# Latent attention: the second key block's values as one product of whole 32-bit operands, and the next head's transposes directly behind the values' product

## The chip, the cores and the metric

The kernel runs on one core of a Trainium2 chip. The metric is the device time of one execution in microseconds (us). The engines are TensorE (PE: matrix products and transposes; PEld: its weight loads), VectorE (DVE), ScalarE (ACT), GpSimd (POOL) and SyncE (SP, which issues the DMAs). Each engine works off its own queue in order and waits on semaphores of the others.

## The reference

A decoder trunk of two layers on 256 tokens of width 1024, all in float32. Layer 0 has a forgetting attention, layer 1 a multi-head latent attention. Around each stand two half-step feed-forward blocks and an input embedding, and behind each part a layer norm. What the change touches is the latent attention of layer 1:

```python
def mla_mixer(x, w_dq, q_norm, w_uq, w_o, k_nope, k_rope, v, cos, sin):
    c_q = rms_norm(x @ w_dq, q_norm)
    q = jnp.einsum('bsc,chd->bshd', c_q, w_uq)
    q_nope = q[..., :QK_NOPE_DIM]
    q_rope = rope(q[..., QK_NOPE_DIM:], cos[:, None, :], sin[:, None, :])
    scale = (QK_NOPE_DIM + QK_ROPE_DIM) ** -0.5
    ...
    # for each block of 128 queries, against the keys up to them:
    s = (einsum('bqhd,bkhd->bhqk', qn, k_nope) + einsum('bqhr,bkr->bhqk', qr, k_rope)) * scale
    w = jax.nn.softmax(where(k_pos <= q_pos, s, -inf), axis=-1)
    o = jnp.einsum('bhqk,bkhd->bqhd', w, v)
    ...
    return o.reshape(B, S, MLA_HEADS * V_HEAD_DIM) @ w_o
```

There are 16 heads with values of width 128, and two blocks of 128 queries. The first block of queries sees the first 128 keys, the second block sees all 256. So of the transposed probabilities there are three 128x128 blocks a head: first keys by both blocks of queries (256 columns), and second keys by the second block of queries (128 columns).

## The kernel before, in words

**Split operands.** A float32 matrix is kept as two parts of the type fp32r: the high part is a copy through that type, the low part is the rest (`parts`, L496 to 500: ScalarE copies, VectorE subtracts). A product is then three passes of TensorE: high by high, high by low, low by high (`mm3`, L481). Weights come by DMA into `raw` and are split in the same way (`Stream.split`: ScalarE writes the high part, VectorE the low part; lines L193, L194, L201, L205).

**The order.** The latent attention (`mla`, L1226) is a list of steps, `ORDER` (L47), run one after the other by the loop at L1504. Each step puts its instructions at the end of the queues of the engines it uses, so the list is the order on every engine. `f n`, `a` and `l` are the weight splits that are put between the steps. The steps that matter, for head h:

- `gen h`: query and key of head h by products with the weights (15 passes of 256 columns), and their split into `qk`.
- `QK h`: the scores of head h into a PSUM bank of the ring `tr` (two banks), ten passes.
- `sm h`: the softmax without its division. VectorE reduces (L1420), ScalarE takes the exponentials into `P` (L1425).
- `div h 0`: VectorE takes reciprocals (L1434) and multiplies both blocks of `P` by them (L1437).
- `T h`: three transposes of `P` on TensorE (L450), and the split of the result into the one tile `PT` (L452).
- `AV h`: the product of values and probabilities (L1462): three passes of 256 columns for the first keys, three of 128 columns for the second keys. Its result is split into `ot`.
- `O h t`: the output projection of head h for the token block t: six passes of 512 columns.
- `V g t`: the values of four heads for the key block t: six passes of 512 columns, and ScalarE's copy of the high part (L1270). `vlo g t` is VectorE's subtraction for the low part (L1275).
- `rc`, `rot`, `zs`, `zU`: rotation, split and transposes of the rotary queries, partly on POOL.

`T h` can run when `div h 0` is done, `AV h` when the split of `PT` is done. `PT` has one buffer, so `T h` follows `AV h-1` in any order.

Of the kernel before, what the change touches and what calls it, by code (L numbers as in the profile page):

```python
# [10 lines left out]
F32 = mybir.dt.float32  # L11
F32R = mybir.dt.float32r
AF = mybir.ActivationFunctionType
# [33 lines left out]
ORDER = (  # L47
# [26 lines left out]
)  # L74


# [14 lines left out]
class Recorder:  # L91
# [10 lines left out]
    lend = reclaim = check = load = busy = pair = split = split_pieces = ahead = later = split_now = fill = pump  # L102
    between, hl, hold = {}, {}, False
# [293 lines left out]
class Trunk:  # L397
# [828 lines left out]
    def mla(self, li):  # L1226
        nc, S, a = self.nc, self.S, self.a
# [4 lines left out]
        v = {}  # L1232
# [26 lines left out]
        vps = {}  # L1259

        def V(g, t):
            w = self.use(("kvv", g))
            ps = vps[g, t] = self.bank(("h", "y", "tr")[VRING[g][t]])
            for k in range(2):
                self.mm3(
                    ps, lambda i: self.ckv[:, i, 256 * k + 128 * t : 256 * k + 128 * t + 128],
                    lambda i: w[:, i, 512 * k : 512 * k + 512], k == 0, k == 1,
                )
            o = v[t, g] = self.tl([128, 2, 512], F32R, "g4", 5)
            nc.scalar.activation(o[:, 0, :], ps, AF.Copy)  # L1270
            S.busy(act=512)

        def vlo(g, t):
# [70 lines left out]
        zT = self.xT.rearrange("p t i k c -> p (t i k c)").rearrange("p (h c) -> p h c", c=256)  # L1344
# [34 lines left out]
        st, PT = {}, {}  # L1379
# [66 lines left out]
        def T(h):  # L1446
            P = st.pop(h)
            b = self.bank("tr")
            for i in range(3):
                self.transpose(b[:, 128 * i : 128 * i + 128], P[:, 128 * i : 128 * i + 128])  # L1450
            o = self.tl([128, 2, 384], F32R, "PT", 1)
            self.parts(o[:, 0, :], o[:, 1, :], b[:, 0:384])
            PT[h] = o

        OT = []

        def ot_of(h):
            if h >= 14:
                return self.kvt[:, 512 * (h - 14) : 512 * (h - 13)].rearrange("p (i c) -> p i c", i=2)
            return OT[h >= 10][:, (h + 2 * (h >= 10)) % 4]  # L1460

        def AV(h):  # L1462
            if h in (0, 10):
                OT.append(self.own([128, 4, 2, 256], F32R, "ota" if h else "otb"))
            o = PT.pop(h)
            ps = self.bank("h")
            g, c = h // 4, 128 * (h % 4)
            for m, (i, jj) in enumerate(((0, 0), (0, 1), (1, 0))):
                self.mm(
                    ps[:, 0:256], v[0, g][:, i, c : c + 128], o[:, jj, 0:256], m == 0, False  # L1470
                )
            for m, (i, jj) in enumerate(((0, 0), (0, 1), (1, 0))):
                self.mm(
                    ps[:, 128:256], v[1, g][:, i, c : c + 128], o[:, jj, 256:384], False, m == 2
                )
            ot = ot_of(h)
            self.parts(ot[:, 0, :], ot[:, 1, :], ps[:, 0:256])

        y = [[None] * 2 for _ in range(2)]
# [14 lines left out]
        def hold(x):  # L1494
            S.hold = bool(x)

        steps = dict(
            dq=dq, rms=rms, dqs=dq_scale, cqT=cq_transpose, V=V, vlo=vlo, qr=q_rope, rope=rope, rc=rope_copy, rot=rotate, zT=zT_first,
            zs=z_split, zU=zT_last, gen=gen, QK=QK, sm=softmax, div=divide, T=T, AV=AV, O=O, y=room, hold=hold,
            f=S.fill, a=S.ahead, l=S.later, XT=lambda t, n: self.XT(t, (n,)),  # L1500
            exp=lambda: self.ready_for(AF.Exp), gb=lambda: self.load_gb(li, 1),
            lend=lambda: S.lend("qk"), ln=lambda t: self.ln(t, y[t], ALPHA, LN_EPS),
# [119 lines left out]
```

## Time and profile before

| what | us |
|---|---|
| median of three runs (1078.75 to 1079.87) | 1078.85 |
| the profiled execution, its own time | 1081.3 |
| its span, first to last instruction | 1079.5 |
| TensorE busy in the span | 1063.7 |
| VectorE busy | 719.1 |
| ScalarE busy | 543.7 |
| POOL busy | 73.2 |

The mean granted clock of TensorE was 0.997 of full speed. The latent attention's heads lie between about 740 and 850 us of the span. In the timeline a row gives the start in us, the time from the first start to the last end of the instructions merged in it, the engine, the line, the operation, output and input, and the count; in brackets stands the idle time before it and what ended it. Matmuls are pipelined: the time between two starts is the cost of one, and it is shorter than the duration shown. Loads of weights overlap the matmuls.

### The profile page before, as it was taken

How to read it: one execution, taken by the hardware profiler on the slowest of the kernel's cores; microseconds unless marked ns; L12 is line 12 of the kernel's file. 1: busy time of each engine (PE TensorE's matmuls, PEld its weight loads, DVE VectorE, ACT ScalarE, POOL GpSimd, SP SyncE). 2: the span in 40 equal slices, each digit the busy share in tenths (PEclk: the TensorE clock that was granted, in tenths of full speed). 3: DMA queues.
4: the chain of work that ended last, by engine and by line, in shares of the span. 5: the costliest groups of instructions: out<-in, count | busy, mean ns of one | idle time of the engine just before them, and what ended most of it. 6: DMA issues, size and time to landing. Idle time of an engine off the chain costs nothing.

```text
span 1079.5 us, 17532 instructions
## 1 busy us (share of the span) xinstructions
PE 1063.7 (99%) x7236; PEld 973.4 (90%) x7236; DVE 719.1 (67%) x1043; ACT 543.7 (50%) x805; POOL 73.2 (7%) x104
## 2 busy tenths in 40 slices
PE   9999999999999999999999999999999999999997
PEld 8989998899889999998899999988899789898986
DVE  6675545888897545548966554388777886455566
ACT  5564433667646434444555443336576465444431
POOL 0000000223200000000320000012100000000000
PEclk9999999999999999999999999999999999999998
DMA  8785642543348655454477554322444468555502
GB/s 297 288 313 207 252 167 81 198 179 130 119 167 303 233 190 193 142 196 161 164 270 273 188 190 158 108 93 106 145 145 164 180 226 311 186 207 189 185 11 78
DMA packets 33091, 199.58 MB, mean 185 GB/s; under 512 B 3698, under 2 KB 5490, under 8 KB 12148
## 3 DMA queue, kind: packets, MB, share of 16 engines
q1 hardware_dynamic: 33012, 198.47, 51.4%
q8 instruction: 57, 0.93, 0.3%
q14 instruction: 22, 0.18, 0.0%
HBM read 197.40 MB, written 1.05 MB: 184 GB/s over the span
## 4 chain that ended last, share of the span: by engine, by line
PE 89%; DVE 6%; ACT 2%; issue 1%; POOL 1%; DMA 0%; SPq 0%; DVEq 0%; POOLq 0%; ACTq 0%
PE y L489 32%; PE h L489 32%; PE tr L489 22%; DVE hl L194 2%; PE tr L493 2%; DVE x L569 1%; ACT hl L193 1%; DVE st L551 0%; DVE x L550 0%; DMA raw<-in_w_dram 0%; PE h L493 0%; ACT P L1425 0%; DVE PT L499 0%; PE tr L1065 0%; DVE g L798 0%
## 5 line engine op out<-in xcount | busy, mean ns | idle before, releaser
L194 DVE TENSOR_TENSOR hl<-raw,hl 128x1024 fp32r<-128x1024 f32 (+3 forms) x268 | 316.0, 1198 | 150.4 <-ACT hl L193 149.6
L193 ACT ACTIVATE hl<-raw 128x1024 fp32r<-128x1024 f32 (+3 forms) x268 | 269.8, 1028 | 184.9 <-PE y L489 98.4
L489 PE MATMUL y<-hl,g 128*128 128x512 f32 x816 | 190.7, 390 | 0.0
L489 PE MATMUL h<-xT,hl 128*128 128x256 f32 x1560 | 188.6, 280 | 1.4 <-ACT hl L231 0.5
L489 PEld LDWEIGHTS h<-xT,hl 128*128 128x128 f32 x1560 | 184.2, 191 | 3.5 <-ACT xT L498 0.9
L489 PEld LDWEIGHTS y<-hl,g 128*128 128x128 f32 x816 | 152.0, 188 | 30.7
L489 PE MATMUL tr<-xT,hl 128*128 128x256 f32 x1512 | 176.6, 277 | 0.0
L489 PEld LDWEIGHTS tr<-xT,hl 128*128 128x128 f32 x1512 | 174.2, 188 | 0.5
L489 PE MATMUL h<-hl,xT 128*128 128x512 f32 (+2 forms) x300 | 67.8, 374 | 0.4 <-DVE xT L499 0.4
L489 PE MATMUL y<-hl,xT 128*128 128x512 f32 (+3 forms) x360 | 65.4, 334 | 0.0
L489 PEld LDWEIGHTS h<-hl,xT 128*128 128x128 f32 x300 | 53.2, 188 | 10.7 <-DVE xT L499 1.0
L489 PEld LDWEIGHTS y<-hl,xT 128*128 128x128 f32 x360 | 55.5, 188 | 6.3 <-ACT xT L498 0.4
L561 POOL TENSOR_TENSOR rs<-ve,mhalf 128x1 f32<-128x1 f32 x16 | 15.2, 951 | 601.3 <-DVE ve L560 601.3
L489 PE MATMUL y<-hl,otb 128*128 128x512 f32 x168 | 43.3, 399 | 0.7 <-DVE hl L194 0.5
L499 DVE TENSOR_TENSOR g<-P,g 128x512 fp32r<-128x512 f32 x38 | 26.3, 692 | 26.5 <-ACT g L498 26.5
L498 ACT ACTIVATE xT<-tr 128x512 fp32r<-128x512 f32 x28 | 16.1, 597 | 49.3 <-PE tr L493 49.3
L498 ACT ACTIVATE g<-P 128x512 fp32r<-128x512 f32 x38 | 24.0, 632 | 32.3 <-DVE P L678 32.3
L489 PEld LDWEIGHTS y<-hl,otb 128*128 128x128 f32 x168 | 30.2, 188 | 7.1 <-DVE hl L194 0.8
L194 DVE TENSOR_TENSOR otb<-raw,otb 128x1024 fp32r<-128x1024 f32 (+1 forms) x20 | 24.1, 1203 | 17.3 <-ACT otb L193 17.3
L677 ACT ACTIVATE P<-tr 128x512 f32<-128x512 f32 x20 | 12.0, 600 | 42.8 <-PE tr L489 42.8
L194 DVE TENSOR_TENSOR qk<-raw,qk 128x1024 fp32r<-128x1024 f32 (+1 forms) x21 | 25.7, 1222 | 11.7 <-ACT qk L193 11.7
L678 DVE TENSOR_TENSOR P<-P,tr 128x512 f32<-128x512 f32 x20 | 13.7, 687 | 28.6 <-PE tr L489 17.0
(264 smaller groups left out, 1414.8 us busy)
## 6 DMA issues: line engine op xcount, KB each, us to landing
raw<-in_ffn_in_dram SPq DMA_DIRECT2D x85, 1024.0 KB, 5.0
raw<-in_ffn_out_dram SPq DMA_DIRECT2D x44, 1024.0 KB, 5.0
raw<-in_pg_dram SPq DMA_DIRECT2D x8, 1024.0 KB, 4.8
raw<-in_mo_dram SPq DMA_DIRECT2D x8, 1024.0 KB, 4.8
raw<-in_kq_dram SPq DMA_DIRECT2D x8, 640.0 KB, 4.0
gb<-in_ln_g_dram SPq DMA_DIRECT2D x8, 512.0 KB, 5.8
gb<-in_ln_b_dram SPq DMA_DIRECT2D x8, 512.0 KB, 6.8
raw<-in_fk_dram SPq DMA_DIRECT2D x4, 1024.0 KB, 4.9
```

The source lines that it names most:

```text
L193: nc.scalar.activation(hi, src, AF.Copy)
L194: nc.vector.tensor_tensor(lo, src, hi.bitcast(F32), op=ALU.subtract)
L489: self.nc.tensor.matmul(out, lhsT, rhs, start=start, stop=stop)
L493: self.nc.tensor.transpose(out, in_, self.ident)
L498: self.nc.scalar.activation(hi, src, AF.Copy)
L499: self.nc.vector.tensor_tensor(lo, src, hi.bitcast(F32), op=ALU.subtract)
L561: nc.gpsimd.tensor_tensor(rs, ve, self.mhalf, op=ALU.pow)
L569: nc.vector.scalar_tensor_tensor(xs, xs, rs if i else mv[:, 0:1], self.gb[:, i, c0:c1], op0=ALU.mult if i else ALU.subtract, op1=ALU.add i ...
L677: nc.scalar.activation(gt, ps[0], AF.Silu)
L678: nc.vector.tensor_tensor(gt, gt, ps[1], op=ALU.mult)
```

## The change

For the second key block, the values stay one plain float32 tile (`V g 1` copies its bank once, and the four steps `vlo g 1` are gone). `T h` splits only the first 256 columns of the transposed probabilities; VectorE copies the last 128 columns as plain float32 into `raw`, which lies in the place of an older tile, `negc`. `AV h` keeps its three passes of 256 columns and then issues one product of the two plain float32 operands in place of three passes of 128 columns.

In `ORDER`, `T h+1` now stands directly behind `AV h` for every head (with `zU 1 1` between them for head 8). Where the two were apart, either `AV h` moved back to the place of `T h+1` (heads 1, 10 and 11: `AV 1` behind `QK 3` and `gen 4`; `AV 10` behind `gen 13`, with `T 11` ahead of `QK 12`; `AV 11` behind `gen 14`), or `T h+1` moved forward (`T 2` ahead of `O 0 0`, `T 3` ahead of `gen 5`, `T 4` ahead of `zU 0 0` and `gen 6`, `T 5` ahead of `O 3 1` and `gen 7`, `T 8` ahead of `gen 10`, `T 9` ahead of `gen 11`, `T 10` ahead of `gen 12`, `T 14` ahead of `O 6 1` and `QK 15`, `T 15` ahead of `O 8 1`, with `O 7 1` now ahead of `AV 14`). The order in the queues of DMAs and of POOL is the same as before, and so is all work outside the latent attention.

```diff
@@ ORDER, the stretch from QK 2 to QK 7 @@
     "f 4", "QK 2", "f 2", "zs 1 0", "y", "sm 2", "a", "f 3", "div 2 0", "O 0 1", "f 1",
-    "AV 1", "f 4", "QK 3", "gen 4", "f 1", "O 0 0", "T 2", "sm 3", "a", "div 3 0", "l", "O 1 0", "O 1 1",
-    "AV 2", "f 4", "a", "f 3", "gen 5", "T 3", "f 4", "l", "QK 4", "sm 4", "f 1", "f 1", "div 4 0", "f 1", "f 3",
-    "f 1", "f 4", "O 2 1", "O 2 0", "AV 3", "f 2", "zU 0 0", "gen 6", "T 4", "a", "QK 5", "sm 5", "f 2", "div 5 0",
-    "f 2", "l", "f 3", "O 3 0", "f 1", "V 2 1", "vlo 2 1", "f 4", "AV 4", "f 4", "O 3 1", "l", "gen 7", "T 5", "a",
+    "f 4", "QK 3", "gen 4", "f 1", "AV 1", "T 2", "O 0 0", "sm 3", "a", "div 3 0", "l", "O 1 0", "O 1 1",
+    "AV 2", "T 3", "f 4", "a", "f 3", "gen 5", "f 4", "l", "QK 4", "sm 4", "f 1", "f 1", "div 4 0", "f 1", "f 3",
+    "f 1", "f 4", "O 2 1", "O 2 0", "AV 3", "T 4", "f 2", "zU 0 0", "gen 6", "a", "QK 5", "sm 5", "f 2", "div 5 0",
+    "f 2", "l", "f 3", "O 3 0", "f 1", "V 2 1", "f 4", "AV 4", "T 5", "f 4", "O 3 1", "l", "gen 7", "a",
     "QK 6", "sm 6", "f 2", "O 4 1", "div 6 0", "l", "f 1", "O 4 0", "f 4", "zU 1 0", "AV 5", "f 4", "T 6", "a",
...
@@ ORDER, the end @@
     "gen 15", "AV 12", "T 13", "sm 14", "f 1", "div 14 0", "l", "O 12 0",
-    "AV 13", "O 6 1", "f 3", "QK 15", "f 3", "T 14", "f 4", "lend", "O 13 0", "sm 15", "f 1", "f 1",
-    "div 15 0", "l", "AV 14", "O 7 1", "hold 0", "O 8 1", "hold 1", "f 3", "gb", "f 1", "T 15", "O 9 1",
+    "AV 13", "T 14", "O 6 1", "f 3", "QK 15", "f 3", "f 4", "lend", "O 13 0", "sm 15", "f 1", "f 1",
+    "div 15 0", "l", "O 7 1", "AV 14", "T 15", "hold 0", "O 8 1", "hold 1", "f 3", "gb", "f 1", "O 9 1",
     "AV 15", "O 14 0", "hold 0", "f 5", "f 3", "O 15 0", "ln 0",
...
@@ def V(g, t) @@
-            o = v[t, g] = self.tl([128, 2, 512], F32R, "g4", 5)
-            nc.scalar.activation(o[:, 0, :], ps, AF.Copy)
+            if t:
+                o = v[t, g] = self.tl([128, 512], F32, "g4", 5)
+                nc.scalar.activation(o, vps.pop((g, t)), AF.Copy)
+            else:
+                o = v[t, g] = self.tl([128, 2, 512], F32R, "g4", 5)
+                nc.scalar.activation(o[:, 0, :], ps, AF.Copy)
@@ def T(h) @@
             o = self.tl([128, 2, 384], F32R, "PT", 1)
-            self.parts(o[:, 0, :], o[:, 1, :], b[:, 0:384])
-            PT[h] = o
+            raw = self.tl([128, 384], F32, "negc", 1)[:, 0:128]
+            self.parts(o[:, 0, 0:256], o[:, 1, 0:256], b[:, 0:256])
+            nc.vector.tensor_copy(raw, b[:, 256:384])
+            S.busy(dve=128)
+            PT[h] = o, raw
@@ def AV(h) @@
-            for m, (i, jj) in enumerate(((0, 0), (0, 1), (1, 0))):
-                self.mm(
-                    ps[:, 128:256], v[1, g][:, i, c : c + 128], o[:, jj, 256:384], False, m == 2
-                )
+            self.mm(ps[:, 128:256], v[1, g][:, c : c + 128], raw, False, True)
+            S.busy(pe=128)
```

More of the change, by code (lines that the diff above doesn't have):

```diff
@@ L1464, in AV @@
                 OT.append(self.own([128, 4, 2, 256], F32R, "ota" if h else "otb"))
-            o = PT.pop(h)
+            o, raw = PT.pop(h)
             ps = self.bank("h")
```

47 rows, old and new, of the table ORDER are left out of this document.

## The prediction

> **What bounds the kernel now.** I read the page's busy times and chain first, then the busy time of each engine stretch by stretch, then the timelines of the three stretches in which TensorE is not full.
>
> ```profile
> span 1079.5 us, 17532 instructions
> PE 1063.7 (99%) x7236; PEld 973.4 (90%) x7236; DVE 719.1 (67%) x1043; ACT 543.7 (50%) x805; POOL 73.2 (7%) x104
> PE 89%; DVE 6%; ACT 2%; issue 1%; POOL 1%; DMA 0%; SPq 0%; DVEq 0%; POOLq 0%; ACTq 0%
> ```
>
> TensorE is the bound: a matmul taken out in a full stretch is time won. The next rows are stretches (us: length, then busy time of PE, PEld, DVE, ACT, POOL) of the latent attention.
>
> ```profile
> 744.00:762.00 18.00, 14.42 (x97) 12.22 (x97) 14.35 (x26) 11.59 (x28) 12.91 (x10) 1.00 0.36 131
> 762.00:832.00 70.00, 70.00 (x494) 65.09 (x493) 55.16 (x135) 44.91 (x104) 0.00 (x0) 1.00 0.41 141
> 832.00:847.00 15.00, 14.40 (x83) 11.76 (x82) 10.77 (x25) 8.76 (x20) 0.00 (x0) 1.00 0.40 141
> ```
>
> In the heads from 762 to 832 TensorE never waits. Before that it loses 3.6 us, after it 0.6 us. So a new wait in the middle costs its whole length, and a matmul saved inside an early wait earns nothing.
>
> **The price of the new values' product.** AV(h) drops three 128-column passes on split operands and issues one product of whole 32-bit operands. The kernel has one such product: the warm-up at L465, 384 columns.
>
> ```profile
> 1.20 0.50 PEld L465 LDWEIGHTS y<-mask 128*128 128x128 f32 x2 [1.20 <-POOL mhalf L449]
> 1.21 1.65 PE L465 MATMUL y<-mask 128*128 128x384 f32 x2 [1.21 <-POOL mhalf L449]
> 2.65 1.06 PE L493 MATMUL tr<-ident 128*128 128x128 f32 x4
> 786.30 0.60 PE L493 MATMUL tr<-ident,ota 128*128 128x128 f32 x4
> ```
>
> One instruction became two weight loads and two passes, and the next one started 1.44 us after it. The two groups of transposes show that everything at the start runs at half speed: 1.06 us for four against 0.60. So 128 columns cost at most 1.44 / 3 / 2 = 0.24 us. The lower end is two weight loads.
>
> ```profile
> 774.14 0.41 PEld L489 LDWEIGHTS tr<-qk 128*128 128x128 f32 x3
> 774.47 0.30 PEld L489 LDWEIGHTS tr<-fs,xT 128*128 128x128 f32 x2
> 786.63 0.77 PEld L489 LDWEIGHTS h<-PT,g 128*128 128x128 f32 x6
> 787.34 0.32 PEld L493 LDWEIGHTS tr<-ident,P 128*128 128x128 f32 x3
> ```
>
> Three 128-column passes take 0.33 us from load to load (774.14 to 774.47), six of AV 0.71. Two loads are 0.22 us, so the new product costs 0.22 to 0.24 and replaces 0.33 to 0.35: 0.09 to 0.13 won a head. I take 0.10, from the cleaner 128-column row. Heads 0 and 1 end ahead of waits that other engines set (below), so 14 heads count: **-1.4 us** (-1.3 to -1.8).
>
> The Trainium skill, "FP8 and Floating Point Precision", section "TensorE Precision Notes", has true FP32 as four passes through the array. The two 384-column passes agree if each makes two of them; a reader who takes it as four loads has the third rival.
>
> **VectorE and ScalarE.**
>
> ```profile
> L1275 DVE TENSOR_TENSOR g<-y,g x3: 678/679/683, 729.7 to 752.5; 128x512 fp32r<-128x512 f32 x3
> L499 DVE TENSOR_TENSOR PT<-tr,PT 128x384 fp32r<-128x384 f32 x16 | 8.8, 550 | 0.3 <-ACT PT L498 0.2
> L233 DVE CAST hl<-raw x1: 293/293/293, 3.8 to 3.8; 128x256 fp32r<-128x256 f32 x1
> ```
>
> Four low parts of second-block values go (4 x 0.68). Each T's subtraction shrinks from 384 to 256 columns (about 0.41) and a copy of 128 is added (under the 0.29 of 256; I take 0.2): +0.06 to +0.12 a head. VectorE gains about 1.3 us in all, off the bound. The one removed ahead of a wait, before T 0, doesn't end it: the division of P does, and that stands in front. ScalarE's copy shrinks by a third, hidden. DMAs, SP's and POOL's queues keep their order.
>
> **The moved transposes.** T(h) needs head h's divided P, and its work used to sit behind a score product, a `gen` (1.8 us) or an `O` (1.4 us). Now it follows AV(h-1), and everything behind it on TensorE waits with it. I went through each head: QK(h), what TensorE has until T(h), and when VectorE ends the division.
>
> *T 2.* AV 1 leaves its place ahead of QK 3, T 2 overtakes O 0 0.
>
> ```profile
> 754.75 3.73 DVE L194 TENSOR_TENSOR hl<-raw,hl 128x512 fp32r<-128x512 f32 x2
> 758.53 1.10 PE L489 MATMUL h<-gb,hl 128*128 128x256 f32 x7 [0.98 <-DVE hl L194]
> 759.46 1.55 PE L489 MATMUL y<-hl,otb 128*128 128x512 f32 x6
> 760.45 0.77 DVE L1437 TENSOR_SCALAR P<-P,su 128x128 f32<-128x128 f32 x2
> 761.11 0.61 PE L493 MATMUL tr<-ident,P 128*128 128x128 f32 x3
> 761.47 0.70 PE L489 MATMUL y<-hl,otb 128*128 128x512 f32 x2
> ```
>
> VectorE's two splits end at 758.5 and hold gen 4, whose end at 759.46 stays; so does the division (760.45 on). Before, O 0 0 ran from 759.46 and T 2 came almost without a wait. After, AV 1 fills 0.6 us, TensorE stands until 761.1, and O 0 0's 1.4 us comes behind. **+1.5 us** (1.3 to 1.6). T 3 and T 4 overtake gen 5 and gen 6; reckoned on from there, AV(h-1) ends within 0.1 to 0.2 us of the division: **+0.2** (0 to 0.5).
>
> *T 5* overtakes O 3 1 and gen 7.
>
> ```profile
> 775.39 1.56 PE L489 MATMUL y<-hl,otb 128*128 128x512 f32 x6
> 777.54 1.57 ACT L193 ACTIVATE hl<-raw 128x1024 fp32r<-128x1024 f32 x2
> 778.17 0.80 PE L489 MATMUL h<-PT,g 128*128 128x256 f32 x6
> 778.62 1.23 DVE L194 TENSOR_TENSOR hl<-raw,hl 128x1024 fp32r<-128x1024 f32 x1 [0.85 <-ACT hl L193]
> 778.81 1.59 PE L489 MATMUL y<-hl,otb 128*128 128x512 f32 x6
> 779.96 0.55 DVE L1437 TENSOR_SCALAR P<-P,su 128x128 f32<-128x128 f32 x2
> 782.04 0.49 PE L493 MATMUL tr<-ident,P 128*128 128x128 f32 x3
> ```
>
> QK 5 ended at 775.39 (O 3 0 begins there), AV 4 at 778.81 (O 3 1 begins). The division starts at 779.96 because a split stands in front of it on VectorE, which itself waits for ScalarE behind the exponentials. P's first block is out about 0.28 later, 4.85 us after QK 5; PT of head 4 now comes earlier and gives 0.4 back. That is 4.45 against 3.3 us of TensorE work: **+1.1** (0.9 to 1.5). T 9 and T 10, by the same reckoning: **+0.4** (0.1 to 0.7).
>
> *T 14* overtakes O 6 1 and QK 15.
>
> ```profile
> 834.96 0.80 PE L489 MATMUL h<-PT,g 128*128 128x256 f32 x6
> 835.60 1.59 PE L489 MATMUL y<-hl,otb 128*128 128x512 f32 x6
> 836.33 0.55 DVE L1437 TENSOR_SCALAR P<-P,su 128x128 f32<-128x128 f32 x2
> 838.18 0.49 PE L493 MATMUL tr<-ident,P 128*128 128x128 f32 x3
> ```
>
> AV 13 ended at 835.60 (O 6 1 begins), P's first block at 836.6: **+1.1** (0.9 to 1.3). T 15 then comes 0.2 late (0 to 0.5). In return two waits for PT go:
>
> ```profile
> 839.90 1.13 PE L489 MATMUL h<-PT,g 128*128 128x256 f32 x6
> 845.37 0.28 PE L489 MATMUL h<-PT,g 128*128 128x256 f32 x1
> 846.06 0.78 PE L489 MATMUL h<-PT,g 128*128 128x256 f32 x5 [0.41 <-DVE PT L499]
> ```
>
> AV 14 took 1.13 against 0.80, and AV 15's second pass came 0.69 after the first against 0.12: **-0.9** (-1.0 to -0.7). T 6, 7, 8, 11, 12 and 13 keep at least 0.1 us in hand. Each new wait also stretches the transposes behind it (0.61 at T 2 against 0.49), 0.12 four times: **+0.5**.
>
> **The sum.** -1.4 + 1.5 + 0.2 + 1.1 + 0.4 + 1.1 + 0.2 - 0.9 + 0.5 = +2.7 us, I take +2.6. Against the profiled execution's 1081.3 us (span 1079.5) that is 1083.9; the median of the runs, 1078.85, lies 2.45 lower, so 1081.45. With every end the same way it runs from about +0.9 to +4.6. 0.2% is 2.16 us, about what a measurement of this kernel tells from no change.
>
> **Rivals.**
>
> *Not slower: the collision at gen 4 goes.* The two splits (512 and 768 columns) took 3.73 us, where 1024 columns take 1.23 at 778.62: 1.5 expected, 2.2 lost while POOL was busy for 12.9 of the 18 us. Should POOL's rotations fall elsewhere, T 2 and gen 4 come up to 2.2 us earlier: +0.4, 1079.2. It decides from 0.5 us on. For it: VectorE is freed of 0.68 us ahead. Against: after that it waits for ScalarE at gen 3 again, so the phase against POOL moves by 0.1 only. The Trainium skill, "GPSIMD Engine Reference", section "1. Specifications", lists this contention for VectorE instructions with two SBUF inputs; the splits are such, and they stay. Chance 0.16.
>
> *Faster: the moved transposes find P ready.* If VectorE runs ahead by 1.4 us from T 2 on, the four waits vanish and -1.4 - 0.9 remain: -2.3, 1076.6. For it: 1.3 us less VectorE work, and PT earlier in its queue. Against: the rows of T 5 and T 14, in which splits and exponentials, untouched, set the division. Chance 0.17.
>
> *Four loads.* Should the whole-operand product load weights four times at 0.11, it costs 0.44 instead of 0.23: +0.21 for 14 heads, +5.6 in all, 1084.4. L465's two loads speak against it. Chance 0.09.
>
> **How the numbers follow.** My forecast has 0.58, with 1080.2 to 1083.3 as its own range (0.07 of it under +2.16). Slower by over 0.2%: 0.51 + 0.09 = 0.60. Within: 0.07 + 0.16 = 0.23. Faster: 0.17. The range 1076.6 to 1083.6 takes in the two better rivals and leaves out the four loads and the outer ends.
>
> **What would show it.** Right: five TensorE instructions an AV, the product's two passes 0.22 to 0.24 us from load to load; waits of about 1 us before T 2, T 5 and T 14, released by the division; no wait in AV 14 and AV 15. Wrong: T 5 or T 14 without a wait, the splits at gen 4 shorter, four loads, or an extra gap where products of the two kinds meet, which no row here shows.

## The result and the profile after

The changed kernel takes 1085.01 us (median of 4 runs, 1084.14 to 1086.95) against 1079.36 for the kernel before, run beside it (4 runs, 1078.75 to 1081.46): a ratio of 1.005, 95% interval 1.0038 to 1.0062, or 5.65 us slower. The prediction was 1081.45, with 1076.6 to 1083.6 as its range. The sign is right and the size is not. Of the 3.56 us between forecast and result, 0.5 lie in the kernel before, which was 1078.85 us when the forecast was made and 1079.36 beside this run; the rest is the change, +5.65 us against +2.6.

The profiled execution took 1085.44 us. Its span and busy times, from the page:

```profile
span 1083.3 us, 17518 instructions
PE 1063.7 (98%) x7220; PEld 971.9 (90%) x7220; DVE 718.9 (66%) x1055; ACT 543.9 (50%) x805; POOL 73.3 (7%) x104
```

TensorE is busy for the same 1063.7 us, and the span has grown by idle time alone. (That the busy time did not fall does not mean that the new product saves nothing. From QK 1 to the end TensorE is busy 326.1 us before, 324.7 with the product alone (the first experiment below), and 326.2 after: the late transposes are stretched, and that counts as busy.) Where the idle time lies shows in the same stretches as before (length, then busy time of PE, PEld, DVE, ACT, POOL); a fourth one is added, first of the kernel after, then of the kernel before:

```profile
744.00:762.00 18.00, 13.08 (x86) 10.75 (x85) 14.83 (x28) 10.54 (x22) 12.93 (x10) 1.00 0.34 123
762.00:832.00 70.00, 68.37 (x468) 62.24 (x467) 52.84 (x141) 44.46 (x102) 0.00 (x0) 1.00 0.39 136
832.00:847.00 15.00, 13.40 (x82) 11.24 (x82) 9.30 (x29) 6.88 (x20) 0.00 (x0) 1.00 0.36 125
847.00:866.00 19.00, 18.02 (x85) 14.62 (x84) 16.60 (x24) 8.48 (x10) 1.05 (x1) 1.00 0.53 184
```

```profile
847.00:866.00 19.00, 18.76 (x87) 15.38 (x86) 16.92 (x26) 7.86 (x11) 1.98 (x2) 1.00 0.57 217
```

TensorE loses 1.3, 1.6, 1.0 and 0.7 us more. The last one was not foreseen.

To follow the time head by head, I take from each profile the start of QK h's first pass and count it from QK 1's. Counting from there is needed because the work before it, which all the kernels share, differs from profile to profile: QK 1 started between 738.30 and 742.32 us. The two rows at each end, of before and after:

```profile
740.95 0.45 PE L489 MATMUL tr<-qk 128*128 128x128 f32 x3
837.03 0.45 PE L489 MATMUL tr<-qk 128*128 128x128 f32 x3
```

```profile
739.92 0.45 PE L489 MATMUL tr<-qk 128*128 128x128 f32 x3
840.84 0.44 PE L489 MATMUL tr<-qk 128*128 128x128 f32 x3
```

From QK 1 to QK 15 it was 96.08 us and is 100.92: 4.84 us more. All profiles in this way, in us against the kernel before (XT: the first transpose of x behind the layer norm; end: the last matmul):

| kernel | QK 4 | QK 5 | QK 6 | QK 9 | QK 14 | QK 15 | XT | end |
|---|---|---|---|---|---|---|---|---|
| after | +1.52 | +1.73 | +3.24 | +2.96 | +3.22 | +4.85 | +4.19 | +4.89 |
| after, second profile (e10_after) | +2.03 | +1.94 | +3.47 | +3.16 | +3.42 | +5.05 | +4.29 | +5.01 |
| product alone (e1_product) | -0.08 | -0.13 | -0.24 | -0.52 | -0.92 | -1.01 | -1.04 | -0.98 |
| product alone, again (e1b_product) | -0.05 | -0.14 | -0.25 | -0.53 | -0.92 | -1.00 | -1.03 | -0.99 |
| order alone (e2_order) | +1.88 | +1.87 | +3.41 | +3.38 | +3.78 | +5.36 | +4.87 | +5.59 |
| AV 1, T 2 back (e3_t2back) | +1.71 | +1.90 | +3.42 | +3.14 | +3.39 | +5.01 | +4.16 | +4.88 |
| AV 1, T 2 back, again (e3b_t2back) | +1.48 | +1.68 | +3.20 | +2.89 | +3.13 | +4.75 | +4.09 | +4.78 |
| AV 1, T 2, T 3, T 4 back (e9_front) | -0.07 | -0.16 | +1.64 | +1.36 | +1.58 | +3.20 | +2.39 | +3.09 |
| T 5 back (e4_t5back) | +1.51 | +1.70 | +1.48 | +1.25 | +1.51 | +3.13 | +2.45 | +3.17 |
| div 5 ahead of its splits (e8_div5) | +1.71 | +1.72 | +1.58 | +1.26 | +1.49 | +3.11 | +2.42 | +3.11 |
| end back (e5_endback) | +1.68 | +1.74 | +3.27 | +2.98 | +3.22 | +3.11 | +3.07 | +3.15 |
| `gb` early (e6_gb) | +1.52 | +1.72 | +3.26 | +3.00 | +3.26 | +4.89 | +4.00 | +4.02 |
| product, old order, two steps moved (e7_best) | -0.07 | -0.17 | -0.27 | -0.53 | -0.92 | -1.00 | -1.02 | -0.96 |

The change costs in jumps: at QK 4, at QK 6, at QK 15 and behind XT. From QK 6 to QK 9 it wins a little in each head (+3.24 to +2.96); from there to QK 14 it loses 0.26 again. These are the rows of TensorE at the jumps, of the kernel after:

```profile
758.46 0.52 PE L489 MATMUL h<-PT,g 128*128 128x256 f32 x3
758.82 0.38 PE L489 MATMUL h<-negc,g 128*128 128x128 f32 x2
760.09 0.61 PE L493 MATMUL tr<-ident,P 128*128 128x128 f32 x3 [0.89 <-DVE P L1441]
...
779.10 0.38 PE L489 MATMUL h<-negc,g 128*128 128x128 f32 x2
780.87 0.61 PE L493 MATMUL tr<-ident,P 128*128 128x128 f32 x3 [1.39 <-ACT hl L193]
...
809.13 0.61 PE L493 MATMUL tr<-ident,P 128*128 128x128 f32 x3 [0.23 <-DVE P L1441]
...
822.92 0.70 PE L493 MATMUL tr<-ident,P 128*128 128x128 f32 x3
...
839.00 0.61 PE L493 MATMUL tr<-ident,P 128*128 128x128 f32 x3 [1.08 <-DVE P L1441]
...
844.73 0.52 PE L489 MATMUL h<-PT,g 128*128 128x256 f32 x3
...
845.84 0.61 PE L493 MATMUL tr<-ident,P 128*128 128x128 f32 x3 [0.37 <-DVE P L1441]
...
849.05 0.52 PE L489 MATMUL h<-PT,g 128*128 128x256 f32 x3
```

The rows with a bracket are T 2, T 5, T 9, T 14 and T 15, each directly behind an AV (T 9 with the four transposes of `zU 1 1` between) and each waiting for the division (`P`, L1441). At T 5 the name in brackets is ScalarE's split at L193, for which the division's own queue had waited. T 11 (822.92) shows no bracket, but its transposes are stretched. AV 14 (844.73) and AV 15 (849.05) run their three passes of 256 columns in 0.52 us, as at 758.46: the waits for `PT` in them are gone. The rows with `negc` are the new product: `negc` is the raw tile, x2 its two passes.

### The profile page after: what moved, and what is told of

The parts are those of the page before. It is cut to its first block, busy times and chain, and to the rows that moved or that the text cites. A ratio compares the mean times of both kernels' runs of the same rounds, so it can differ in the third digit from the quotient of the medians.

```text
span 1083.3 us, 17518 instructions
## 1 busy us (share of the span) xinstructions
PE 1063.7 (98%) x7220; PEld 971.9 (90%) x7220; DVE 718.9 (66%) x1055; ACT 543.9 (50%) x805; POOL 73.3 (7%) x104
## 4 chain that ended last, share of the span: by engine, by line
PE 88%; DVE 6%; ACT 2%; issue 1%; DMA 1%; POOL 1%; SPq 0%; DVEq 0%; ACTq 0%; POOLq 0%
PE y L489 32%; PE h L489 31%; PE tr L489 22%; PE tr L493 2%; DVE hl L194 2%; DMA gb<-in_ln_b_dram 1%; DVE x L569 1%; ACT hl L193 1%; ACT P L1429 1%; DMA raw<-in_w_dram 0%; PE h L493 0%; DVE tr L1424 0%; DVE P L1441 0%; DVE x L550 0%; DVE st L551 0%
## 5 line engine op out<-in xcount | busy, mean ns | idle before, releaser
L193 ACT ACTIVATE hl<-raw 128x1024 fp32r<-128x1024 f32 (+3 forms) x268 | 269.9, 1029 | 185.6 <-PE y L489 98.6
```

The source lines that it names most:

```text
L193: nc.scalar.activation(hi, src, AF.Copy)
```

## The experiments

**The product and the order apart.** The first kernel keeps the new code of `V`, `T` and `AV` and takes the old order; the second does the reverse.

```diff
 e1_product: ORDER as before, without "vlo 0 1", "vlo 1 1", "vlo 2 1", "vlo 3 1"; V, T, AV as after
 e2_order:   ORDER as after, with the four "vlo g 1" at their old places; V, T, AV as before
```

> The new values' product alone: the changed code of V, T and AV with the old order of the steps (only the four `vlo g 1` are gone). Theory, 'the parts add up': each AV saves the 0.10 us a head that the changed kernel's trace shows (two passes of 0.109 us in place of three of 0.11), every wait stays as it was before, and the time falls by 1.4 us (1.0 to 1.9), PE busy in 762 to 832 stays 70.0 (no wait). Rival, 'the product brings a wait of its own' (VectorE's copy of 0.28 us behind the subtraction, on which the last pass of AV depends, or the tile `raw`): AV's last pass starts late in some heads, and the time is the same or up to 2 us longer. In that case the order costs less than the difference of the two kernels (5.65 us).

> The new order of the steps alone, with the old values' product (split second-block values, three passes of 128 columns; the four `vlo g 1` stand at their old places). Theory, 'the parts add up': the order costs the 5.65 us between the two kernels plus the 1.4 us that the product wins, so +7.0 us (6.0 to 8.0) against the kernel before; waits of about 1 us at T 2, 1.5 at T 5, 1.2 at T 14, 0.5 at T 15 and 1 us at the layer norm behind the attention. Rival, 'the product sets the waits' (VectorE's new copy or the missing `vlo` shift VectorE's queue so that T 5 comes late): T 5's wait is 1.1 us or less here and the order alone costs 5.6 us or less.

The product alone is 0.98 us faster by the trace, ratio 0.9988 (0.9978 to 0.9998), the lower end of what the theory allowed (1.0 to 1.9). It brings no wait of its own. The order alone is 5.59 us slower by the trace, ratio 1.0047 (1.0031 to 1.0063). T 5's jump (QK 5 to QK 6) is 1.54 us with the old product and 1.51 with the new one, so the product does not set the waits, and that rival falls. But +7.0 falls too, for two reasons. The trace holds 4.89 us of the 5.65 between the medians, and in the new order the product wins 0.6 to 0.7 us and not 1.4: 5.59 - 4.89 = 0.70, and 5.59 - 5.01 = 0.58 against the second profile of the changed kernel, in which the clock fell for a stretch as it did in that of e2_order (last section). What the product saves ahead of a wait, the wait takes. The times alone do not tell the two orders' kernels apart (1.0047 with the old product, 1.005 and 1.0057 with the new one).

**T 5: where it stands, and what it waits for.** The first kernel puts T 5 back behind `gen 7`. The second leaves TensorE's order alone and moves VectorE's division of head 5.

```diff
 e4_t5back
-"AV 4", "T 5", "f 4", "O 3 1", "l", "gen 7", "a",
+"AV 4", "f 4", "O 3 1", "l", "gen 7", "T 5", "a",
 e8_div5
-"QK 5", "sm 5", "f 2", "div 5 0", "f 2",
+"QK 5", "sm 5", "div 5 0", "f 2", "f 2",
```

> The changed kernel with T 5 behind gen 7, as before (so behind O 3 1 too); the rest stays. Theory, 'each wait is paid once': the wait of 1.55 us and 0.12 us of stretched transposes go, QK 6 starts 1.6 us earlier than in the changed kernel, and the end is 1.3 to 1.7 us earlier: +3.2 to +3.6 from 637 us on. Rival, 'the wait only moves': T 6, T 9 and T 11 wait longer by what was won, and the end is less than 0.8 us earlier.

> The changed kernel with the step `div 5 0` moved ahead of the two weight splits (1024 columns each, 1.22 and 1.23 us of VectorE, the second behind 0.85 us of waiting for ScalarE) that stand between the softmax's reductions and the division of head 5; TensorE's order does not change. It asks what makes T 5 late. Theory, 'the splits in front of the division': VectorE divides about 1.3 us after its reductions instead of 3.2, so P is ready before AV 4 ends, T 5 waits 0.1 us or less, its three transposes take 0.22 us from first to last start instead of 0.34, and QK 6 starts 1.4 to 1.7 us earlier. Rival, 'the exponentials set it': the division waits for ScalarE until about 780 us anyway, and T 5 still waits 1 us. Second rival, 'the splits are needed as early as they are': O 3 1 or gen 7 waits for its weights in place of T 5, and QK 6 starts less than 0.8 us earlier.

With T 5 back, QK 6 starts 1.76 us earlier than in the changed kernel and the end comes 1.72 us earlier: the wait is paid once and does not move on to a later head. Moving the division gives the same without touching T 5 (1.66 at QK 6, 1.78 at the end; ratio to before 1.0033, 1.0018 to 1.0047). The rows of VectorE and TensorE, first after, then with the division moved:

```profile
776.00 1.55 PE L489 MATMUL y<-hl,otb 128*128 128x512 f32 x6
777.03 1.22 DVE L205 TENSOR_TENSOR hl<-raw,hl 128x1024 fp32r<-128x1024 f32 x1
779.10 1.23 DVE L194 TENSOR_TENSOR hl<-raw,hl 128x1024 fp32r<-128x1024 f32 x1 [0.85 <-ACT hl L193]
780.44 0.55 DVE L1441 TENSOR_SCALAR P<-P,su 128x128 f32<-128x128 f32 x2
```

```profile
777.29 0.55 DVE L1441 TENSOR_SCALAR P<-P,su 128x128 f32<-128x128 f32 x2
777.76 1.22 DVE L205 TENSOR_TENSOR hl<-raw,hl 128x1024 fp32r<-128x1024 f32 x1
778.05 0.38 PE L489 MATMUL h<-negc,g 128*128 128x128 f32 x2
778.27 0.49 PE L493 MATMUL tr<-ident,P 128*128 128x128 f32 x3
```

In the changed kernel two splits stand ahead of the division. Moved to the front, it is done before AV 4 ends, and T 5 follows AV 4's two last passes at once (778.05 to 778.27, 0.22 us). So the splits in the queue made T 5 late, as the prediction had it, and nothing waits for them in its place.

**T 2 and T 3.** The first kernel puts AV 1 and T 2 back; it was run twice. The second puts T 3 and T 4 back as well.

```diff
 e3_t2back, e3b_t2back
-"f 1", "f 4", "QK 3", "gen 4", "f 1", "AV 1", "T 2", "O 0 0",
+"f 1", "AV 1", "f 4", "QK 3", "gen 4", "f 1", "O 0 0", "T 2",
 e9_front, besides
-"AV 2", "T 3", "f 4", "a", "f 3", "gen 5",   ...  "AV 3", "T 4", "f 2", "zU 0 0", "gen 6",
+"AV 2", "f 4", "a", "f 3", "gen 5", "T 3",   ...  "AV 3", "f 2", "zU 0 0", "gen 6", "T 4",
```

> The changed kernel with AV 1 ahead of QK 3 and T 2 behind O 0 0, as before; the rest stays. Counted from 637 us on, where the work before the latent attention is behind, the changed kernel's last matmul is 4.87 us later than that of the kernel before. Theory, 'each wait is paid once': TensorE waits for VectorE at gen 4 and T 2 and nothing later depends on it, so QK 4 starts 1.6 us earlier than in the changed kernel and the end is 1.6 us earlier too (1.4 to 1.7): +3.3. Rival, 'the wait only moves': VectorE's queue is what is late, so a TensorE that arrives earlier waits longer at T 5, T 9 or T 14, and the end is less than 0.8 us earlier.

> The kernel of the run with AV 1 and T 2 put back, once more. In that run TensorE's granted clock was 0.50 for 3.41 us from 756.9 on, just where O 0 0 and T 2 stand, and O 0 0's six passes came every 0.427 us instead of 0.232; QK 4 started 1.69 us later than in the kernel before. Theory, 'each wait is paid once, and the slow clock hid it': without the slow clock QK 4 starts 0.1 us early to 0.2 us late against the kernel before (the late 0.2 from T 3, which stays ahead of gen 5), and the last matmul is +3.1 to +3.4 from 637 us on. Rival, 'the wait only moves to T 3': with the clock full, QK 4 is again 1.5 us late. Should the slow clock come again, it follows a stretch in which TensorE waits at gen 4, and the run tells only that.

> The changed kernel with AV 1, T 2, T 3 and T 4 put back to their places before the change, so that from QK 2 to QK 5 the order is the old one; T 5 and all behind it stay moved. Theory, 'each wait is paid once': QK 5 starts 0.1 us earlier than in the kernel before (the product alone gave 0.13), T 5 waits 1.5 us again and QK 6 starts 1.4 us late, and the last matmul is +3.0 us from 637 us on (2.8 to 3.3) with the clock full throughout. Rival, 'VectorE is late as a whole': T 5 now waits 2.3 us or more, because TensorE arrives 1.8 us earlier at a VectorE that does not, and the end is +4 us or more.

The first run changed nothing (+1.71 at QK 4), but TensorE ran at half its clock just there (see the last section), so it decided nothing. The second had the full clock, and again nothing was won: +1.48. The rival is right. The wait moves to T 3, as TensorE's rows of the second run show:

```profile
760.48 0.61 PE L493 MATMUL tr<-ident,P 128*128 128x128 f32 x3
760.84 3.00 PE L489 MATMUL y<-hl,otb 128*128 128x512 f32 x12
763.68 0.52 PE L489 MATMUL h<-PT,g 128*128 128x256 f32 x3
764.04 0.38 PE L489 MATMUL h<-negc,g 128*128 128x128 f32 x2
765.60 0.61 PE L493 MATMUL tr<-ident,P 128*128 128x128 f32 x3 [1.18 <-DVE P L1441]
```

T 3 stands directly behind AV 2 and starts 1.56 us after its last pair of passes (764.04), where two passes take 0.22: a wait of 1.34 us that the changed kernel does not have there. With T 3 and T 4 back too, the jump is gone (-0.07 at QK 4) and the end comes 1.80 us earlier. So T 3's move alone costs as much as both moves together: VectorE is late for head 3 as for head 2, and in the old order `gen 5` hides it at T 3. Whether T 2's move alone would cost the same was not tried. T 5 then waits a little more than in the changed kernel (QK 5 to QK 6: 1.80 against 1.51), far from the second rival's 2.3.

**The end of the attention.** The first kernel puts T 14, AV 14 and T 15 back. The second moves only the step `gb`, whose two DMAs bring the next layer norm's gain and bias.

```diff
 e5_endback
-"AV 13", "T 14", "O 6 1", "f 3", "QK 15", "f 3", "f 4", ... "O 7 1", "AV 14", "T 15", "hold 0", "O 8 1", "hold 1", "f 3", "gb", "f 1", "O 9 1",
+"AV 13", "O 6 1", "f 3", "QK 15", "f 3", "T 14", "f 4", ... "AV 14", "O 7 1", "hold 0", "O 8 1", "hold 1", "f 3", "gb", "f 1", "T 15", "O 9 1",
 e6_gb
-"QK 15", "f 3", "f 4", "lend", ... "hold 1", "f 3", "gb", "f 1",
+"QK 15", "gb", "f 3", "f 4", "lend", ... "hold 1", "f 3", "f 1",
```

> The changed kernel with the end of the order put back: T 14 behind QK 15, AV 14 ahead of O 7 1, T 15 behind O 8 1 and the split, all as before; the rest of the change stays. Theory, 'the end also makes the layer norm late': the waits at T 14 (1.25 us) and T 15 (0.53) and 0.65 us of the wait at the layer norm go, with 0.2 us of stretched transposes, and the two waits for PT (0.9 together) come back: 1.5 to 1.9 us less than the changed kernel, so 3.7 to 4.2 us over the kernel before; the second DMA of `gb` is issued about 4 us earlier. Rival, 'the layer norm's wait has come from elsewhere' (whatever delays the heads before 830 us): only 1.0 us less than the changed kernel, and the wait of 1.05 us at the transposes of x stays.

> The changed kernel with the step `gb` (two DMAs of the layer norm's gain and bias) moved from behind the last split up to behind QK 15, so that on SP's queue it stands ahead of the load of `raw` that waits for a buffer. Nothing else moves. Theory, 'gain and bias come late': the wait of 1.3 us of VectorE for `gb` at L569 goes, TensorE's wait before the transposes of x falls from 1.05 us to 0.4 or less, and the time falls by 0.6 to 1.0 us against the changed kernel. Rival, 'the layer norm's own chain sets it' (VectorE's statistics and POOL's root): VectorE reaches L569 no earlier, the wait stays near 1 us, and the time is the same within 0.2 us.

With the end put back, the last matmul is 1.74 us earlier than in the changed kernel, as the theory had it (1.5 to 1.9; ratio to before 1.0028, 1.0017 to 1.0039), and from XT to the end 0.08 us are lost instead of 0.70: the wait at the layer norm came from the end of the order. `gb`'s second DMA is issued 2.5 us earlier, counted from QK 1, not the 4 expected; that was enough. With only `gb` moved, 0.87 us are won, 0.19 of them already at XT (ratio to before 1.0035, 1.0021 to 1.0049). The chain of waits of the kernel after shows how the delay travels (start, length, what):

```profile
845.41 0.30 DVE P L1441
845.71 0.14 issue
845.84 0.62 PE tr L493 x3
...
846.55 0.39 ACT PT L498
846.94 0.95 ACT hl L193
...
847.92 1.23 DVE hl L194
849.14 1.15 DVE qk L194
...
850.30 0.33 SPq L363
...
850.70 0.42 SPq L419
...
851.17 7.34 DMA gb<-in_ln_b_dram
...
858.64 1.42 DVE x L569 x2
```

T 15 waits for its probabilities; the copy of its result (`PT`) stands on ScalarE ahead of a weight split, so that split and the next one on VectorE are late; the load into `raw` waits on SP's queue for the buffer that they free; and the DMAs of `gb` stand behind that load. The last takes 7.34 us to land, and VectorE reaches L569 first. With `gb` early VectorE's wait for it (1.30 us) is gone; 0.44 us of waiting for POOL's root are left, as in the kernel before. These are the rows of VectorE and TensorE, after and with `gb` early:

```profile
858.64 0.75 DVE L569 SCALAR_TENSOR_TENSOR x<-x,rs,gb 128x512 f32<-128x512 f32 x1 [1.30 <-DMA gb<-in_ln_b_dram]
860.99 0.63 PE L493 MATMUL tr<-ident,x 128*128 128x128 f32 x4 [0.89 <-DVE x L569]
```

```profile
859.60 0.75 DVE L569 SCALAR_TENSOR_TENSOR x<-x,rs,gb 128x512 f32<-128x512 f32 x1 [0.44 <-POOL rs L561]
861.94 0.63 PE L493 MATMUL tr<-ident,x 128*128 128x128 f32 x4 [0.27 <-DVE x L569]
```

**A version that beats both?** The product in the old order, with AV 14 behind O 7 1 and `gb` early. T 15, too, stands a little earlier in the list, ahead of `hold 1`, `f 3` and `f 1`, which the expectation does not name.

```diff
 e7_best, against e1_product
-"QK 15", "f 3", "T 14", ... "AV 14", "O 7 1", "hold 0", "O 8 1", "hold 1", "f 3", "gb", "f 1", "T 15",
+"QK 15", "gb", "f 3", "T 14", ... "O 7 1", "AV 14", "hold 0", "O 8 1", "T 15", "hold 1", "f 3", "f 1",
```

> The new product with the old order and two steps of the end moved: AV 14 behind O 7 1 (as in the changed kernel, so that it finds its PT ready) and `gb` behind QK 15. Theory: the product's 1.0 us, plus AV 14's wait of 0.33 us where PT comes late; `gb` wins nothing here, since the layer norm's own chain ends last (TensorE waits 0.28 us for x, VectorE 0.44 us for POOL's root, nobody for `gb`): -1.3 us from 637 us on, ratio about 0.9987. Rival, 'the end is set by VectorE': AV 14's 0.33 us comes back as a longer wait at AV 15 (0.58 us now), because T 15's split stands behind two weight splits whose time does not move: -1.0 us, no better than the product alone.

> The product alone in the old order, once more, for a ratio beside that of the changed kernel on one chip. The traces of the first run gave -0.98 us from 637 us on. Theory, 'the gain is what the trace shows': ratio 0.9985 to 0.9996. Rival, 'the first interval (0.9978 to 0.9998) was the luck of the draw, and no gain can be measured': 0.9996 to 1.0005.

> The changed kernel itself, once more, beside the product alone. Theory, 'the time is what the trace shows': +4.87 us from 637 us on in the trace, ratio 1.0040 to 1.0050. Rival, 'the timed runs hold more than that trace, because the clock falls to half in some of them': ratio 1.0050 to 1.0065.

The rival is right: -0.96 by the trace, no better than the product alone, ratio 1.0001 (0.9992 to 1.001). AV 14 no longer waits, but AV 15 now waits 0.92 us for `PT` instead of 0.58. T 15's split still stands on VectorE behind the same two weight splits (they start at 841.87 and 843.01, the split of `PT` at 844.15), in spite of T 15's new place in the list. The product alone, run again, gave -0.99 by the trace and 0.999 (0.9979 to 1.0001). Its gain is 1 us in both traces, and just at the edge of what the times can tell. It is the best version found, and it beats both kernels by the trace. The changed kernel, run again, gave +5.01 by the trace and a ratio of 1.0057 (1.0045 to 1.007), or about 6 us. Its times lie somewhat above its traces. The ratio lies where the rival put it, but the rival's reason is not shown: the profile in which the clock fell has only 0.12 us more than the other (+5.01 against +4.89). The intervals reach down to the traces' 4.9, and whether the rest is more than scatter stays open.

## Why the prediction was right and wrong

The step that failed is the one that put everything outside the heads at nothing: "DMAs, SP's and POOL's queues keep their order". In its place the runs showed a wait of the layer norm for `gb` that costs 0.87 us (e6_gb). Three terms of the sum were also mis-sized: the product, T 5, and the end of the heads. With every term at its outer end the prediction came to +4.6; the trace has +4.89, and with `gb` early +4.02. So without the wait for `gb` the time comes out inside the range by its ratio (1.0035 times 1078.85 is 1082.6, though the interval reaches to 1084.1), and still 1.2 us over the forecast.

The product alone sets off what belongs to the order: each row of the table minus that of e1_product. Beside it stand the terms of the prediction, each with the 0.12 that it gave to a stretched transpose.

| step | predicted | measured |
|---|---|---|
| the product | -1.4 | -0.98 |
| T 2 (to QK 4) | +1.62 | +1.60 |
| T 3, T 4 (to QK 5) | +0.2 | +0.26 |
| T 5 (to QK 6) | +1.22 | +1.62 |
| T 9, T 10, measured with T 11 (to QK 14) | +0.4 | +0.66 |
| T 14, T 15, less the waits in AV 14, AV 15 (to XT) | +0.64 | +1.09 |
| layer norm behind (to the end) | 0 | +0.64 |
| sum | +2.7 | +4.9 |

- **The bound and the sign: right.** The time that was added is idle time of TensorE, and the new waits stand at T 2, T 5 and T 14, released by the division. AV 14 and AV 15 no longer wait.
- **The product's price: right; its count: mis-sized.** The new product makes two loads and two passes, 0.109 us from start to start. It follows the passes on split operands without a gap (the rows at 758.46 and 758.82: three passes of 0.12), and the four-load rival falls. A head wins 0.10 us where no wait follows: 0.68 for the seven AVs between QK 6 and QK 14. But 14 heads were counted. Of the first three AVs 0.08 is left at QK 4, since the waits at `gen 4` and T 2 take the rest, and from QK 14 to XT, where the last heads wait for `PT`, 0.12 is won. "Heads 0 and 1 end ahead of waits that other engines set" held for more heads than those.
- **T 5: mechanism right, 0.4 too small.** Two parts of its working fail. "PT of head 4 now comes earlier and gives 0.4 back" gave 0.13: QK 5 ends at 776.00 and the division starts at 780.44, 4.44 us later, where it was 4.57; the reductions already followed QK 5 closely, and behind them the two splits and the wait for ScalarE are as long as before. And P's first block is of use to TensorE 0.43 us after the division's start (780.44 to 780.87), not 0.28. The chain above shows the same at T 15: 0.30 for the first block, 0.14 until TensorE has it. That 0.15 was missing at T 5 and at T 14, whose division starts at 838.57 and which starts at 839.00; the term for T 2 had been read off a row of TensorE and did not lack it.
- **T 2 and T 3: right sum, incomplete picture.** The sum took T 2 as the cost and T 3 as a remainder. The experiment shows one lateness of VectorE that either move lays bare.
- **T 9 to T 13: too small.** T 9 waits (0.23 us idle in its row at 809.13), T 10 does not. T 11, which was said to keep 0.1 us in hand, came without any: its three transposes take 0.70 us in their row, against 0.49 where nothing is late.
- **The layer norm: not seen.** "DMAs, SP's and POOL's queues keep their order" is true, and was taken to mean that they cost nothing. A queue that keeps its order still passes on a delay. This is the largest single omission. The table has 0.64 of it; e6_gb, which moves nothing else, gives 0.87 back, and the 0.19 of that at XT are part of the row above. In the chain it begins at T 15, which waited 0.53 us against 0.2 predicted and whose copy now stands ahead of a weight split; which of the two made `gb` late was not separated.
- **The collision at gen 4: stayed, as forecast.** The two splits took 3.72 us, as before, so that rival falls; so does the one in which the transposes find P ready:

```profile
753.75 3.72 DVE L194 TENSOR_TENSOR hl<-raw,hl 128x512 fp32r<-128x512 f32 x2
```

The sum was 2.2 us short of the trace: 0.64 the layer norm, 0.45 the end, 0.42 the product, 0.40 T 5, 0.26 the heads from 6 on. The range had room for some of these together, but none for a wait outside the heads. By the times the change costs another 0.8 us (5.65 against 4.89), for which no cause was found.

## What to carry to other kernels

When an instruction is moved ahead of work that used to cover its input, price it from the producer's whole queue, and count the time from the start of the producer to the consumer's start as a trace shows it, not the producer's duration. Follow each new wait also along the queues that keep their order: here a late copy on ScalarE delayed a split, the split a buffer, the buffer a load, and the load a DMA that a stage 13 us later needed. A saving of a tenth of a microsecond a head counts only in heads that no wait ends; and where two moves lay bare the same lateness, undoing one of them wins nothing.

## What the runs showed that was not expected

TensorE's granted clock fell to half in the middle of some kernels, for one stretch of 3.41 us, always at `gen 4` and T 2 (profiles of e2_order, e3_t2back, e5_endback, e8_div5 and e10_after; not in the other eight of the changed forms, nor in that of before). The rows are stretches of e3_t2back, then of the same kernel run again (e3b_t2back); the number behind POOL's is the granted clock:

```profile
753.49:756.90 3.41, 1.77 (x12) 1.57 (x13) 3.32 (x6) 0.65 (x2) 3.33 (x3) 1.00 0.51 182
756.90:760.31 3.41, 3.41 (x13) 2.72 (x11) 2.45 (x6) 2.60 (x7) 1.53 (x2) 0.50 0.88 305
```

```profile
755.42:758.83 3.41, 1.90 (x14) 1.70 (x15) 3.18 (x6) 0.79 (x2) 3.41 (x2) 1.00 0.50 185
758.83:762.24 3.41, 3.31 (x17) 2.44 (x16) 2.59 (x6) 2.74 (x8) 1.41 (x2) 1.00 0.88 308
```

Ahead of the fall TensorE was busy for 1.77 of 3.41 us, 52%, in pieces (the longest idle time that its rows name there is 0.98 us); in the repeat it was 1.90, 56%, and the clock stayed. The times between two changes of the clock are whole multiples of 3.413 us in every profile (750.93 and 317.44 in e3_t2back, 220 and 93 of them), so the stretches can be laid out in a profile without a fall as well. On that grid the share ahead of a fall was 37, 39, 42, 52 and 53%. But it was 54% in e3b_t2back (the stretch shown lies 0.06 us late), 51% in the profile of the changed kernel (1.75 us from 756.76 on) and 44% near the end of e1_product (1.50 us from 1066.33 on), each time without a fall behind it. So a fall came only behind stretches that were about half idle or more, and the busy share, counted to ends of matmuls that are modelled, does not settle which of them. The Trainium skill, "TensorE: Matmul & The Clock Gate", section "What's actually happening", has a free-running window of 3413 ns and a fall after an idle one. The length of the stretch agrees. Here a half-busy window was enough in five profiles, which that section does not say. The same kernel fell in one profile and not in another, although in e3_t2back and e3b_t2back the stretches lie within 0.1 us of each other, counted from QK 1; what decided it stays open. The price was small where TensorE was waiting anyway (0.16 to 0.51 us at QK 4: e5_endback and e10_after against after). In e3_t2back O 0 0 ran at half the clock, and a shorter wait at T 3 took that up.
